# Starting the modulation strips at the tenth instead of the sixth unit of a hybrid encoder's first layer

## Chip, cores and metric

The kernel runs on one core of a Trainium2 chip. The metric is device time in microseconds (us), from the start of the program to its end. TensorE (PE in the rows) does the matmuls; PEld is its weight load, VectorE is DVE, ScalarE is ACT, GpSimd is POOL, and SP is the sequencer whose queue issues nearly all DMAs.

## What is computed

A trunk of two layers over 1024 tokens of width 1024. Layer A is a gated DeltaNet mixer (chunked recurrence, 16 value heads of 128), layer B is attention with forget gates. Each layer is normalised and modulated by three vectors, shift, scale and gate, that come from the conditioning vector `c`. Cut to what matters here:

```python
cond = silu(c)
for i in range(2):
    mod = cond @ ada_w[i] + ada_b[i]            # ada_w[i] is 1024 x 3072
    shift, scale, gate = split(mod, 3)
    h = rmsnorm(x, norm_w[i]) * (1 + scale) + shift
    y = gdn_mixer(h, ...) if i == 0 else fox_mixer(h, ...)
    x = x + gate * y
return rmsnorm(x, final_norm_w)
```

Shift and scale of layer A are needed at once. The gate of layer A is needed first in layer A's output projection; shift and scale of layer B when its norm starts; the gate of layer B only at the kernel's end.

## The kernel before

**Units.** Layer A is worked in 16 units: two halves of 512 tokens, and in each half eight groups of two value heads. `proj_all` runs over the units. In each it projects k, q and two v tiles, and from the second group of a half on also two z tiles of the group before (four in the last group). A projection tile (`proj_tile`) is 24 matmuls of 128x512: the eight parts of the depth, three products each (high times high, high times low, low times high), since every operand is kept as a rounded high part and a remainder. Behind the projections run, for several units at once, the convolution, transposes, the inversion of triangular blocks (`invert_blocks`, `invert_merge`, partly by way of DRAM: tiles `lb`, `lr`, `rb`, `rmat`), the recurrence (`chain`) and `finish`, which stores the unit's output to `og_d` and `ogl_d`.

**Weights.** In the first half the weights are loaded raw and split by ACT (`whi`, line 337) and DVE (`wlo`, line 340), and all but the first three tiles are stored to DRAM (`wc`, line 809). In the second half those 45 tiles are read back ready (line 418). Between the halves `load_norm` splits the second half's activations. The output projection `out_proj_a` splits its own weights again and loads its rows `ohi` and `olo` (line 450) four steps ahead.

**Strips.** `ada_all` computes what is left of the modulation in eight strips of 512 columns: two for the gate of layer A, two each for shift, scale and gate of layer B. A strip (`ada_strip`, lines 271 to 315) loads a piece of the bias (line 273) and eight pieces of `ada_w` of 128x512 into the two buffers `nx` (line 279), and sums them on DVE into one `nh` buffer, weighted by the conditioning column (line 284 for the first, line 286 for the other seven, line 290 for the bias). Then matmuls with a column of ones sum over the partitions into a bank `mm` of PSUM, one of the two that the projections use as well. Strips of shift and scale are copied to `scol` and `gcol` (line 304); strips of a gate go through `nh` (line 313) to `gate_d` in DRAM (line 315).

**Order.** PE's order is written out by hand: a planner, `Flow`, keeps a clock of its own, and generators yield how long they want to wait. Whoever is due and has the lowest priority number goes on. The strips have priority 6, the projections 9; a strip yields `ADP` = 3500 ns after each of nine loading steps and four times that before its matmuls, so its length in the planner's time doesn't depend on where it runs. The other engines' orders, SP's queue included, are made by the scheduler from the program's order and the priorities. What starts the strips is one condition:

```python
def ada_all():
    yield from hold(lambda: done["kp"] >= AD0 + 1)
    ...
    for _ in range(2):
        nc.vector.tensor_copy(al([P, KT], "nx", 2), ts[AD0]["k"][:, 0, 0:KT])
    for l, cl in strips:
        yield from ada_strip(...)
```

`done["kp"]` is raised when a unit's k tile has been projected. The two small copies (line 1283) make the first two loads wait for that tile on the chip too.

Of the kernel before, what the change touches and what calls it, by code (L numbers as in the profile page):

```python
# [88 lines left out]
Y_N2 = 8500  # L89
Y_N3 = 8500  # L90
ADP = 3500
AD0 = 5
R_AD = 600
R_AS = 2500
R_OA = 1150
# [100 lines left out]
def tile_trunk(  # L196
# [154 lines left out]
    def hold(ok):  # L351
        while not ok():
            yield 300
# [177 lines left out]
    with ExitStack() as sa:  # L531
# [744 lines left out]
        def ada_all():  # L1276
            yield from hold(lambda: done["kp"] >= AD0 + 1)
            def al(shape, name, bufs):
                t = at([P, D], name, bufs) if name == "nx" else at([P, 512], name, bufs)
                return t[0 : shape[0], 0 : shape[1]]  # L1280
# [4 lines that stand above are left out]
                yield from ada_strip(  # L1285
                    al, acc_bank, l, cl, 512, ("nx", 2), ("nh", 2), ("nh", 2), 1, ADP
                )
# [656 lines left out]
```

## Time and profile before

| | us |
|---|---|
| median of 3 runs | 1947.3 |
| lowest and highest | 1943.26, 1947.73 |
| the profiled execution, whole | 1945.78 |
| its span (first to last instruction) | 1943.8 |

The profiled execution lies 1.5 us under the median. The rows below are of that execution and count from the start of its span. In them a busy time with (x) gives the number of instructions behind it, PEclk is the mean granted clock of TensorE as a share of 2.4 GHz, and DMA is the mean busy share of 16 DMA engines.

### The profile page before, as it was taken

To read this page: it belongs to the slowest core of one execution; us is meant where nothing else is said; L and a number is where in the kernel's file an instruction comes from. 1 tells how busy PE (TensorE), PEld (TensorE's weight loads), DVE (VectorE), ACT (ScalarE), POOL (GpSimd) and SP (SyncE) were. 2 spreads that over 40 slices of the span, in tenths; PEclk is the share of its full clock that TensorE was granted. 3 is DMA by queue.
4 is the path that set the end of the run, shared out by engine and by line. 5 is a ranking of instruction groups with operands and counts; after the bars stand their busy time and mean duration, and the time that the engine had idled before them with its cause. 6 is when DMAs were issued, how large, how long until landed. Compare 5 with 4: busy or idle time off the path is not lost.

```text
span 1943.8 us, 35877 instructions
## 1 busy us (share of the span) xinstructions
PE 1828.4 (94%) x12888; PEld 1524.4 (78%) x12888; DVE 1328.3 (68%) x3323; ACT 1033.3 (53%) x2674; POOL 367.0 (19%) x402
## 2 busy tenths in 40 slices
PE   6989999999899999999899799999999999999798
PEld 4767778777787878878776578798988988989576
DVE  5677888788786777776665585475665656656764
ACT  4565566565564555555444453465565555655631
POOL 1100110101210110010001244223223132221222
PEclk7889999899999999999999899999999999999899
DMA  7576767667656565454689982112021011112423
GB/s 270 187 229 205 233 210 245 207 212 249 229 181 186 173 192 176 148 172 138 206 268 320 356 303 98 31 48 66 24 65 60 23 60 45 44 55 71 155 87 95
DMA packets 224985, 307.16 MB, mean 158 GB/s; under 512 B 100460, under 2 KB 136940, under 8 KB 224808
## 3 DMA queue, kind: packets, MB, share of 16 engines
q1 hardware_dynamic: 223800, 304.65, 48.4%
q8 instruction: 101, 1.65, 0.4%
q14 instruction: 76, 0.62, 0.1%
q10 hardware_dynamic: 1008, 0.23, 0.1%
HBM read 223.15 MB, written 81.67 MB: 157 GB/s over the span
## 4 chain that ended last, share of the span: by engine, by line
PE 62%; DMA 14%; DVE 13%; ACT 4%; issue 3%; POOL 1%; SPq 1%; ACTq 0%; DVEq 0%; POOLq 0%
PE mm L137 39%; PE lg L137 5%; PE su L137 4%; PE pt L141 3%; PE oT L137 3%; DMA nx<-in_ada_w_dram 3%; PE tr L141 3%; PE ch L137 2%; DVE wlo L340 2%; PE co L137 2%; DVE cv_y L833 2%; DMA ohi<-og_d 2%; DMA rmat<-rb 1%; DMA wraw<-in_wb_dram 1%; ACT whi L337 1%
## 5 line engine op out<-in xcount | busy, mean ns | idle before, releaser
L137 PE MATMUL mm<-ht_h,whi 128*128 128x512 f32 x768 | 342.4, 446 | 0.5 <-DVE nh L313 0.5
L137 PE MATMUL mm<-ht_h,wlo 128*128 128x512 f32 x768 | 305.2, 397 | 0.0
L137 PE MATMUL mm<-ht_l,whi 128*128 128x512 f32 x768 | 304.3, 396 | 0.8 <-POOL ht_l L340 0.8
L137 PE MATMUL mm<-whi,h_h 128*128 128x384 f32 x512 | 186.7, 365 | 0.9 <-DVE kn L1533 0.9
L137 PE MATMUL mm<-wlo,h_h 128*128 128x384 f32 x512 | 172.6, 337 | 0.6 <-POOL wlo L340 0.6
L137 PEld LDWEIGHTS mm<-ht_h,wlo 128*128 128x128 f32 x768 | 146.3, 190 | 33.9
L137 PE MATMUL mm<-whi,h_l 128*128 128x384 f32 x512 | 172.7, 337 | 0.0
L1684 DVE TENSOR_TENSOR ptl<-pt,pth 128x512 fp32r<-128x512 f32 x192 | 106.4, 555 | 92.5 <-ACT pth L1683 90.5
L137 PEld LDWEIGHTS mm<-ht_h,whi 128*128 128x128 f32 x768 | 147.2, 192 | 28.4 <-issue 1.7
L137 PEld LDWEIGHTS mm<-ht_l,whi 128*128 128x128 f32 x768 | 147.7, 192 | 25.2 <-POOL ht_l L340 1.2
L1683 ACT CAST pth<-pt 128x512 fp32r<-128x512 f32 x192 | 91.3, 477 | 139.8 <-PE pt L141 139.0
L833 DVE SCALAR_TENSOR_TENSOR cv_y<-cv_t,conv_h,cv_y 128x512 f32<-128x512 f32 x192 | 144.4, 752 | 17.3 <-ACT cv_y L825 15.6
L1648 ACT ACTIVATE lg<-lg,mx 128x896 f32<-128x896 f32 (+7 forms) x128 | 99.5, 777 | 54.3 <-DVE mx L1640 48.6
L1527 POOL TENSOR_TENSOR rs<-ss,mhalf 128x4 f32<-128x4 f32 x64 | 64.5, 1007 | 330.8 <-DVE ss L1525 325.2
L340 DVE TENSOR_TENSOR wlo<-ht_h,whi 128x512 fp32r<-128x512 f32 x124 | 93.3, 792 | 47.3 <-ACT whi L337 45.1
L337 ACT CAST whi<-ht_h 128x512 fp32r<-128x512 f32 x124 | 70.7, 618 | 86.5 <-PE mm L137 38.6
L137 PE MATMUL mm<-h_h,whi 128*128 128x512 f32 x240 | 100.5, 419 | 0.7 <-DVE wlo L1783 0.3
L137 PEld LDWEIGHTS mm<-whi,h_h 128*128 128x128 f32 x512 | 97.8, 191 | 3.5 <-ACT v L1529 1.2
L137 PEld LDWEIGHTS mm<-wlo,h_h 128*128 128x128 f32 x512 | 97.2, 190 | 2.8 <-POOL wlo L340 0.8
L141 PE MATMUL pt<-ident,lg 128*128 128x128 f32 (+1 forms) x584 | 96.0, 273 | 3.1 <-ACT lg L1648 3.1
L137 PEld LDWEIGHTS mm<-whi,h_l 128*128 128x128 f32 x512 | 96.4, 188 | 0.0
L137 PE MATMUL mm<-h_h,wlo 128*128 128x512 f32 x240 | 94.9, 395 | 0.0
(390 smaller groups left out, 4492.9 us busy)
## 6 DMA issues: line engine op xcount, KB each, us to landing
ht_h<-in_wa_o_dram SPq DMA_DIRECT2D x62, 512.0 KB, 5.2
wc<-whi SPq DMA_DIRECT2D x45, 512.0 KB, 4.5
wc<-wlo SPq DMA_DIRECT2D x45, 512.0 KB, 4.3
wlo<-wc SPq DMA_DIRECT2D x45, 512.0 KB, 4.9
whi<-wc SPq DMA_DIRECT2D x45, 512.0 KB, 3.6
wlo<-in_wa_c_dram SPq DMA_DIRECT2D x35, 512.0 KB, 4.3
nx<-in_ada_w_dram SPq DMA_DIRECT2D x64, 256.0 KB, 3.4
wraw<-in_wb_dram SPq DMA_DIRECT2D x56, 256.0 KB, 2.8
```

Of the source, the lines that this page charges most:

```text
L137: self.nc.tensor.matmul(out, lhsT, rhs, start=start, stop=stop)
L141: self.nc.tensor.transpose(out, src, ident)
L337: nc.scalar.copy(hi, src)
L340: (lo_eng or nc.gpsimd).tensor_tensor(lo, src, hi.bitcast(F32), op=ALU.subtract)
L833: nc.vector.scalar_tensor_tensor(y, raw[:, j : j + HALF], w[:, j : j + 1], y, op0=ALU.mult, op1=ALU.add)
L1527: nc.gpsimd.tensor_tensor(rs, ss, mhalf[:, 0:4], op=ALU.pow)
L1648: nc.scalar.activation(lg, lg, AF.Exp, scale=-1.0, bias=mx[:, hh : hh + 1], accum_out=sums[:, tt : tt + 1],)
L1683: nc.scalar.copy(ph_[:, cs], pp[:, cs])
L1684: nc.vector.tensor_tensor(pl_[:, cs], pp[:, cs], ph_[:, cs].bitcast(F32), op=ALU.subtract)
```

## The change

`AD0` goes from 5 to 9. The strips start when the k tile of the tenth unit (the second of the second half) has been projected, and not that of the sixth. What a strip does, the strips' order and their pace stay as they are.

```diff
 ADP = 3500
-AD0 = 5
+AD0 = 9
 R_AD = 600
```

## Rows read from the trace of the kernel before

**Rows 1.** The page: span, and the busy time of the busiest engine

```profile
span 1943.8 us, 35877 instructions
PE 1828.4 (94%) x12888; PEld 1524.4 (78%) x12888; DVE 1328.3 (68%) x3323; ACT 1033.3 (53%) x2674; POOL 367.0 (19%) x402
```

**Rows 2.** By stretch: length, busy PE, PEld, DVE, ACT, POOL; PEclk, DMA, GB/s

```profile
152.00:325.00 173.00, 166.87 (x1523) 136.53 (x1522) 140.08 (x398) 107.54 (x317) 20.11 (x39) 0.99 0.67 215
274.00:325.00 51.00, 49.21 (x464) 40.24 (x462) 41.94 (x119) 35.09 (x104) 5.11 (x13) 1.00 0.76 237
325.00:562.00 237.00, 221.13 (x1941) 179.60 (x1940) 194.36 (x479) 140.96 (x417) 33.86 (x47) 0.96 0.68 220
562.00:785.00 223.00, 216.44 (x1941) 176.35 (x1940) 168.38 (x469) 117.29 (x363) 24.11 (x33) 0.99 0.61 187
785.00:946.00 161.00, 159.45 (x1447) 130.08 (x1446) 113.41 (x318) 87.16 (x273) 13.11 (x19) 1.00 0.45 137
946.00:1010.00 64.00, 58.73 (x474) 47.20 (x473) 35.19 (x70) 30.14 (x79) 4.63 (x3) 0.92 0.87 285
1010.00:1100.00 90.00, 74.42 (x329) 57.63 (x328) 51.11 (x88) 37.45 (x84) 12.75 (x10) 0.97 0.97 333
```

**Rows 3.** The strips: loads, sums, matmuls and copies of gates, first and last start

```profile
L279 SPq DMA_DIRECT2D nx<-in_ada_w_dram x64: 327/333/1427, 325.7 to 754.0; - x64
nx<-in_ada_w_dram SPq DMA_DIRECT2D x64, 256.0 KB, 3.4
L286 DVE SCALAR_TENSOR_TENSOR nh<-nx,cond,nh x56: 733/748/780, 331.4 to 758.3; 128x512 f32<-128x512 f32 x56
L137 PE MATMUL mm<-nh,ones x8: 590/590/591, 380.1 to 790.4; 128*1 128x512 f32 x8
L313 DVE COPY nh<-mm x4: 669/671/671, 381.5 to 791.8; 1x512 f32<-1x512 f32 x4
```

**Rows 4.** Timeline of DVE: the k tiles of the sixth and tenth unit

```profile
L840 DVE SCALAR_TENSOR_TENSOR k<-cv_t,cv_y x1: 692/692/692, 324.8 to 324.8; 128x512 f32<-128x512 f32 x1
561.38 0.69 DVE L840 SCALAR_TENSOR_TENSOR k<-cv_t,cv_y 128x512 f32<-128x512 f32 x1
```

**Rows 5.** DVE's busy time by stretch, of line 286 alone, then line 290

```profile
325.00:562.00 237.00, 20.93 (x28) 0.96 0.68 220
562.00:790.00 228.00, 20.93 (x28) 0.99 0.61 188
325.00:562.00 237.00, 2.71 (x4) 0.96 0.68 220
```

**Rows 6.** DVE and POOL busy by stretch, of the splits of line 340 alone

```profile
325.00:562.00 237.00, 34.66 (x50) 5.50 (x4) 0.96 0.68 220
562.00:785.00 223.00, 5.47 (x8) 0.00 (x0) 0.99 0.61 187
```

**Rows 7.** Three short stretches of units 6 to 10 at a lower PEclk

```profile
346.00:357.00 11.00, 10.05 (x78) 7.75 (x81) 9.67 (x23) 5.74 (x22) 2.57 (x1) 0.53 0.66 231
421.00:429.00 8.00, 6.06 (x49) 5.18 (x50) 6.44 (x26) 4.28 (x16) 0.00 (x0) 0.57 0.48 180
595.00:599.00 4.00, 3.50 (x11) 2.89 (x12) 3.77 (x15) 3.87 (x15) 0.00 (x0) 0.57 0.60 230
```

**Rows 8.** PE's longest waits from 325 to 562: total us, times, longest

```profile
PE su L137 <- DVE tmat L1223: 3.6, 4, 2.2
PE tr L141 <- ACT rmat L1218: 3.0, 1, 3.0
```

**Rows 9.** Waits of SP's queue at the strips' loads, 321 to 800

```profile
SPq L279 <- DMA nx<-in_ada_w_dram: 24.6, 18, 3.5
SPq L279 <- DVE nh L286: 24.0, 31, 3.1
```

**Rows 10.** Two short stretches of the output projection, columns as in rows 2

```profile
980.00:995.00 15.00, 15.00 (x92) 12.10 (x91) 9.72 (x18) 6.42 (x17) 2.98 (x2) 1.00 0.72 219
1085.00:1100.00 15.00, 5.41 (x23) 4.18 (x23) 5.23 (x11) 5.23 (x11) 2.60 (x3) 0.79 1.04 405
```

**Rows 11.** PE's waits at the output projection's row loads, 946 to 985

```profile
PE mm L137 <- DMA ohi<-og_d: 4.9, 2, 2.7
```

## Prediction

> **What bounds the kernel now.** I read the page first: PE is busy for 94% of the span, DVE for 68% [rows 1]. So time can only come out of what PE still loses, and that is read by stage. The view by stretch gives it: length less PE's busy time is idle time, and a granted clock under 1.00 is lost time beside it. The stretches are cut at the edges that the change moves: 325, where the strips start, right behind the k tile of the sixth unit [rows 3, 4]; 562, the k tile of the tenth unit [rows 4]; about 790, where the strips end [rows 3]; 946, where the output projection begins.
>
> From 325 to 562 PE is idle for 237 - 221.1 = 15.9 us [rows 2]. The clock is down in two places, 11 us at 0.53 and 8 us at 0.57 [rows 7], which loses 11 x 0.47 + 8 x 0.43 = 8.6 us more (the mean clock of 0.96 in rows 2 agrees: 9.5). Together 24.5 us. From 785 to 946, with neither strips nor many splits, PE is idle for 1.6 us of 161 at full clock [rows 2]. PE's waits say what is late in the first of these stretches: not weights or strips but DVE and ACT work of the recurrence and the inversion (tmat, rmat) [rows 8]. These are short operations that stand in line behind others; DVE is busy for 194.4 of 237 us there (82%), against 113.4 of 161 (70%) from 785 on [rows 2]. Part of that DVE line is the strips, and part the splits of weights, 34.7 us up to 562 and only 5.5 us in the 223 us behind [rows 6].
>
> **The change part by part.** *What moves.* Of eight strips, four run before 562 and four behind it: 28 sums of line 286 in either stretch, 20.9 us each [rows 5]. With four bias additions (2.7 us [rows 5]) some 24 us of DVE's work leave the first stretch, besides four first products and small copies of under 1 us each. On SP's queue 32 loads of 256 KB leave it, with the 0.33 us that issuing one takes and the waits in front of them. POOL and ACT have nothing of it. On PE a strip is two to four short matmuls (0.59 us each for a gate [rows 3]), the same in either place: nothing.
>
> *What the first half gains.* The strips' four units are compared with stretches without strips before them, where splits of weights run too. From 152 to 325: 6.1 us idle and a clock of 0.99, so 1.7 us more, 7.8 us in 173; for 237 us that makes 10.7 and a gain of 24.5 - 10.7 = 13.8. That stretch still holds the norm of the second half's tokens; its last 51 us, from 274, lose 1.8 us, which for 237 us is 8.3 and a gain of 16.2. By PE's instructions per us [rows 2]: 1941/237 = 8.19 with strips, 1523/173 = 8.80 and 464/51 = 9.10 without; the 1941 would take 220.5 or 213.3 us, a gain of 16.5 or 23.7. I take **16 us**, where three of the four stand close together. From below: if a strip costs here only what it costs in the second half (next paragraph), the gain is 4 x 1.6 = 6.4. From above: 23.7.
>
> *What the second half pays.* The first four strips now fall where the last four were, units ten to thirteen, and change nothing there. The next three fall into 785 to 946. The price of one: from 562 to 785 PE is idle for 6.6 us and loses 4 x 0.43 = 1.7 at a low clock [rows 2, 7], 8.3 in all; at the rate of 785 to 946 (1.6 in 161) it would be 2.2. So four strips cost 6.1, 1.5 each; by instructions, 1941/8.99 = 215.9 against 223, so 1.8 each. Three at 1.6: **4.8 us**. The bounds: nothing, since DVE has 30% free; or 3 x 4 = 12, if each costs what it costs in the first half (16 / 4).
>
> *Where the last strip falls.* Strips five to eight took from 562 to 792, 57 us each [rows 3]. Starting at 562 - 16 = 546, eight of them end near 1002. The output projection then starts near 946 - 16 + 5 = 935, so the eighth strip loads from about 945 on, within the projection's first 60 us; the trace of before shows no strip there. Its price has two parts. First, DMA: up to eight loads, 2.1 MB. In 946 to 1010 the queues move 285 GB/s and are busy for 87% [rows 2]; at that rate 2.1 MB take 7.4 us if nothing gives way, and nothing if they fit into the free share (13% of 64 us is 8 us; 980 to 995 is busy for 72% only [rows 10]). PE waits for row loads there already, 4.9 us [rows 11]. I take 3 us, nearer to the free share, since the loads of a strip spread over some 20 us. Second, the bank: the strip is of a gate, and from its matmul at 790.0 to the end of the copy at 792.5 [rows 3] an `mm` bank is held for 2.5 us. The output projection holds both banks for 16 steps at a time and then needs both again, so between 0 and 2.5 us; I take 1.5. Together **4.5 us**, between 0 and 10.
>
> The Trainium skill, "DMA: Bandwidth & Descriptors", section "Where 436 GB/s comes from", puts what one core gets from HBM at about 358 GB/s; by it 2.1 MB more in a full stretch would cost an estimated 5.9 us, and the sum below would be 3.8 us in place of 6.7. The trace shows 405 GB/s from 1085 to 1100 [rows 10], so the limit doesn't hold as stated here.
>
> *Waits.* None is added, but the strips' loads stand in SP's queue, which is in order. They held it for 24.6 + 24.0 us over eight strips [rows 9], 6.1 us a strip. In the second half the ready-made weights and the inversion's small transfers stand behind them, in the output projection the row loads. For the former it is in the 1.6 us above, for the latter it is the second rival. The strips have time: layer A's gate is ready near 546 + 114 = 660, well before 935; shift and scale of layer B near 890, before its norm. What is late next in the first half are the splits, and the same DVE and ACT operations with less in front of them.
>
> *The sum.* -16 + 4.8 + 4.5 = **-6.7 us**. The profiled execution took 1945.8, so 1939.1 for one like it; it lies 1.5 us under the median of the runs, so against the median **1940.6**. About 0.3% (5.8 us) is what a measurement of this kernel can tell from no change, so the forecast lies just beyond that.
>
> **Rivals.** (1) *The first half's stalls aren't the strips'.* Units six to ten also hold four z tiles in unit eight and the splits of the second half's activations, and the waits of rows 8 are for the inversion. Then the gain is the lower bound, 6.4: -6.4 + 4.8 + 4.5 = +2.9, 1950.2. For it: no wait of PE there names a strip's sum. Against: unit five, with the same splits and no strip, loses a third.
>
> (2) *The output projection pays, and the kernel is slower.* The eighth strip's loads get into SP's queue between row loads that are only four steps ahead. PE then waits for the 6.1 us that a strip holds the queue, and such waits lower the clock: in 946 to 1010 it is at 0.92, 5.1 us lost, beside 4.9 us of waiting [rows 2, 11], so about as much again. With DMA's 7.4 and the bank's 2.5 that is 22, and -16 + 4.8 + 22 = +10.8, 1958. It decides from 16 - 4.8 + 5.8 = 17 us on for this one strip. For it: DMA at 87 to 97% and a PE that waits for it. Against: by 945 half of the burst of the start is over. The limit of the Trainium skill's page named above ("DMA: Bandwidth & Descriptors", same section) points this way, but not so far.
>
> (3) *The gain is larger.* The first half reaches the rate of unit five (23.7), and the last strip hides in DMA's free share: -23.7 + 4.8 + 0 = -18.9, 1928.4. For it: unit five is the nearest neighbour. Against: 51 us are a short sample.
>
> (4) *The strips don't leave the line but change it.* PE's order is written out again from the planner's clock; if new waits come up elsewhere for those that go, the sum is near nothing, 1947.
>
> **How the numbers follow.** Forecast 0.46 (its own range is 1933 to 1946, so 0.33 of it faster, 0.13 the same); rival 1 0.18 (0.12 the same, 0.06 slower); rival 2 0.18, slower; rival 3 0.13, faster; rival 4 0.05, the same. Faster 0.46, the same 0.30, slower 0.24. The range of 8 in 10 takes in most of rival 3 and of rivals 1 and 2 up to half of the second's excess: 1929 to 1953.
>
> **What would show it.** Right: line 279 starts near 546 and ends near 960 to 975; the stretch between the k tiles of units six and ten is near 221 us, with DVE's share near 75% and at most one short stretch of half clock; 785 to 946 has 4 to 6 us of idle PE in place of 1.6. Wrong: that first stretch still at 230 us or more (rival 1); waits for ohi of over 10 us, or for an `mm` bank, in the first 60 us of the output projection (rival 2); the stretch at 214 (rival 3).

## The result and the profile after

The changed kernel takes 1958.6 us (median of 5 runs, 1951.2 to 1962.7), the kernel before 1945.7 us (median of 5 runs) beside it: a ratio of 1.0056 with an interval from 1.0035 to 1.0077, so 0.56% slower. Measured side by side once more, later, they came out 0.87% apart (1.0069 to 1.0105). The prediction was 1940.6 us and faster; the measured time lies above its range.

The page says where not to look: PE's busy time hardly changed [rows 1], so what was added is waiting and clock.

```profile
span 1957.3 us, 35882 instructions
PE 1834.7 (94%) x12888; PEld 1527.3 (78%) x12888; DVE 1333.3 (68%) x3323; ACT 1031.3 (53%) x2674; POOL 362.1 (19%) x402
```

The strips' loads now run from 547 to 992, where they ran from 326 to 754 [rows 3]; the last gate's copy (line 313) starts at 1033.9 and not at 791.8. The last line is the store of the output projection's result, whose last start was 1196.2 in the trace of before.

```profile
L279 SPq DMA_DIRECT2D nx<-in_ada_w_dram x64: 328/333/1032, 546.9 to 992.4; - x64
L313 DVE COPY nh<-mm x4: 669/672/679, 602.7 to 1033.9; 1x512 f32<-1x512 f32 x4
L526 SPq DMA_DIRECT2D x_d<-ht_l x8: 319/330/418, 1033.2 to 1212.6; - x8
```

How far the kernel is ahead or behind is read at one operation of each unit, the last step of the k tile (line 840) in DVE's timeline. The tenth unit's, which stood at 561.38 [rows 4], and the sixteenth's, which stood at 891.58:

```profile
545.52 0.68 DVE L840 SCALAR_TENSOR_TENSOR k<-cv_t,cv_y 128x512 f32<-128x512 f32 x1
...
900.42 0.69 DVE L840 SCALAR_TENSOR_TENSOR k<-cv_t,cv_y 128x512 f32<-128x512 f32 x1 [0.78 <-ACT cv_t L837]
```

So the new kernel is 15.9 us ahead at the tenth unit and 8.8 us behind at the sixteenth: it loses 24.7 us on the way, 12.5 of them up to the fourteenth unit (785 in before, 782 in after). At the last store of the output projection it is 16.4 us behind, at the end of the span 13.5. The 15.9 is one trace: in fifteen traces of kernels with no strip before the tenth unit (this one and those below, without one that is 54 us late from its start on) that tile stands between 542.1 and 551.0, which is 10 to 19 us ahead.

The same by stretch (columns as in [rows 2]; the edges are the same k tiles, and 960 on is the output projection):

```profile
273.00:328.00 55.00, 51.03 (x469) 41.14 (x468) 42.50 (x119) 35.43 (x105) 5.22 (x13) 1.00 0.69 224
328.00:546.00 218.00, 209.15 (x1921) 171.50 (x1920) 168.78 (x431) 139.88 (x413) 29.72 (x47) 1.00 0.61 197
546.00:782.00 236.00, 222.08 (x1950) 180.28 (x1948) 175.46 (x480) 118.01 (x371) 21.65 (x34) 0.98 0.59 181
782.00:901.00 119.00, 111.39 (x973) 91.71 (x974) 85.11 (x226) 58.60 (x185) 10.05 (x15) 0.96 0.56 173
960.00:1024.00 64.00, 60.27 (x422) 48.25 (x422) 40.78 (x78) 29.28 (x75) 4.63 (x3) 0.95 0.94 314
```

From 328 to 546 PE is idle for 8.9 us at full clock (before: 15.9 idle and 8.6 for the clock). From 546 to 782 it is idle for 13.9 us and the clock is at half in three stretches of 3.4 us, 5.1 us lost: 19.0 together, where before lost 8.3. From 782 to 901 it is 7.6 idle and one stretch of 10.2 us at half clock, 12.7 together, where the like stretch of before (785 to 892) lost 1.6. DVE is busy for 74 and 72% in these two; in the first half before it was 82%, so DVE's busy share alone doesn't say where PE stalls.

PE's waits from 546 to 960 (us in total, times, longest): the recurrence's state update, 1.0 us in before's 562 to 946, has become the first.

```profile
PE ch L137 <- DVE state L1095: 12.9, 6, 4.3
PE su L137 <- DVE tmat L1248: 3.6, 2, 2.9
PE tr L141 <- ACT rmat L1218: 3.5, 2, 1.9
```

DVE's own waits there: the strips' sums for their loads. In before's second half, with four of the eight strips, they are 10.9 us in 10 waits, for all eight 20.2 in 18; so they hardly grew.

```profile
DVE nh L286 <- DMA nx<-in_ada_w_dram: 22.5, 21, 3.0
```

SP's at the same loads: for the landing of the load before in the buffer, for a sum, and at the end of a strip for the copy behind its matmul.

```profile
SPq L279 <- DMA nx<-in_ada_w_dram: 19.6, 14, 4.3
SPq L279 <- DVE nh L286: 14.8, 21, 1.3
SPq L279 <- DVE scol L304: 14.1, 2, 7.6
```

The longest of PE's waits shows how these hang together in this trace. First DVE's timeline (start, length), then PE's, then the clock:

```profile
793.25 0.16 DVE L965 TENSOR_TENSOR wn<-wn,rk 128x8 f32<-128x8 f32 x1
796.38 0.75 DVE L286 SCALAR_TENSOR_TENSOR nh<-nx,cond,nh 128x512 f32<-128x512 f32 x1 [2.97 <-DMA nx<-in_ada_w_dram]
...
799.20 0.74 DVE L286 SCALAR_TENSOR_TENSOR nh<-nx,cond,nh 128x512 f32<-128x512 f32 x1
799.86 0.60 DVE L1095 SCALAR_TENSOR_TENSOR state<-state,g_ex,co 128x128 f32<-128x128 f32 x2
```

```profile
795.88 0.39 PE L137 MATMUL mm<-ht_h,wlo 128*128 128x512 f32 x1
800.60 1.19 PE L137 MATMUL ch<-state,k 128*128 128x256 f32 x2 [4.33 <-DVE state L1095]
```

```profile
799.90:810.10 10.20, 9.50 (x85) 7.48 (x86) 6.95 (x16) 4.35 (x15) 0.00 (x0) 0.50 0.60 158
```

DVE stands for 2.97 us at a sum whose load hasn't landed; the state update is behind it in DVE's order, and PE waits for that 4.33 us, of which the late load can be at most 2.97 (other operations and one more sum stand in between). Around the end of that wait PE's granted clock falls to 0.50, the lower level of 1.2 GHz, for 10.2 us. Wait and clock together cost near 9 us.

It isn't a single case. Of the six waits for the state update, four, with 11.3 of the 12.9 us, have such a late sum less than 6 us before them. The second trace of the same kernel has late sums before the waits at the same four places; its longest:

```profile
617.62 0.75 DVE L286 SCALAR_TENSOR_TENSOR nh<-nx,cond,nh 128x512 f32<-128x512 f32 x1 [3.19 <-DMA nx<-in_ada_w_dram]
...
619.69 1.18 PE L137 MATMUL ch<-state,k 128*128 128x256 f32 x2 [4.06 <-DVE state L1095]
```

This suggests a theory: strips cost by sums that wait in DVE's queue. It is tested below, and doesn't hold as the whole.

In the output projection the row loads are waited for less than before (4.9 us for `ohi`, [rows 11]); columns as above, 946 to 985:

```profile
PE mm L137 <- DMA olo<-ogl_d: 2.0, 1, 2.0
PE mm L137 <- DMA ohi<-og_d: 0.4, 1, 0.4
```

### The profile page after: what moved, and what is told of

It is laid out like the page before. It is cut to its first block, busy times and chain, and to the rows that moved or that the text cites. A ratio compares the mean times of both kernels' runs of the same rounds, so it can differ in the third digit from the quotient of the medians.

```text
span 1957.3 us, 35882 instructions
## 1 busy us (share of the span) xinstructions
PE 1834.7 (94%) x12888; PEld 1527.3 (78%) x12888; DVE 1333.3 (68%) x3323; ACT 1031.3 (53%) x2674; POOL 362.1 (19%) x402
## 5 line engine op out<-in xcount | busy, mean ns | idle before, releaser
L137 PEld LDWEIGHTS mm<-wlo,h_h 128*128 128x128 f32 x512 | 97.3, 190 | 2.2 <-POOL wlo L340 0.2
```

What stands on the lines that cost most here:

```text
L137: self.nc.tensor.matmul(out, lhsT, rhs, start=start, stop=stop)
```

## The experiments

Each ratio is to the kernel before, run beside it on the same chip, with its 95% interval; 0.1% is 1.9 us. Runs of one kernel on one chip spread by 0.3 to 0.4% to either side, and one profile can differ from the next by 7 us (the two spans of the changed kernel are 1957.3 and 1964.1), so sizes are taken from the ratios, places from the traces. The same pair of kernels came out at 1.0056 and at 1.0087: a difference of two ratios that is below some 0.3% says nothing. Rows of waits are from 546 to 960 (us in total, times, longest) unless it is said otherwise. The edits are to the kernel after unless it is said otherwise.

**No strips.** Takes the whole cost of the strips out.

```diff
-for l, cl in strips:
-    yield from ada_strip(...)
+g = al([1, 512], "nh", 2)
+nc.vector.memset(g, 0.5)
+for l in range(2):
+    for c in range(2):
+        nc.sync.dma_start(gate_d[l : l + 1, c * 512 : c * 512 + 512], g)
+nc.vector.memset(scol[1], 0.1)
+nc.vector.memset(gcol[1], 1.0)
```

> The changed kernel with no strips at all: no loads of ada_w, no sums, no matmuls of strips; the gates and layer B's shift and scale are constants, so the output is not the reference's. It is the floor: before less this is what eight strips cost when begun at the sixth unit, after less this what they cost when begun at the tenth. By the prediction's prices (16 + 6 for before) about 1924. If strips cost in the second half what the second half lost in the changed kernel (25 us from the tenth unit's k tile to the sixteenth's, 8 more in the output projection), about 1925 as well, with the first half like the changed kernel's (221 us from the sixth to the tenth k tile) and the second like that of before without its strips (53 us per unit).

Measured: 0.9951 (0.9935 to 0.9968). The eight strips cost 0.49%, some 9.6 us, started at the sixth unit, and 1.05% (20.5 us), by the second measurement 1.36% (26.5 us), started at the tenth. The tenth k tile is 11.4 us ahead of before and the sixteenth 11.5: the second half without strips runs as long as before's did with four of them.

**Sums without loads.** Every strip adds up the first two pieces again; 62 of 64 loads are gone, all sums, matmuls and copies stay.

```diff
-w = alloc([P, width], ...)
-nc.sync.dma_start(w, ada_w[...])
-ws.append(w)
+if len(fixed) < 2:
+    w = alloc([P, width], ...)
+    nc.sync.dma_start(w, ada_w[...])
+    fixed.append(w)
+ws.append(fixed[kk % 2])
```

> The changed kernel with all sums and matmuls of the strips, in the same order for PE's planner, but only two pieces of ada_w are loaded, and every sum reads one of these two; the output is not the reference's. No sum can wait for a load any more. Theory 'queue' (a sum that waits for its load holds DVE's queue, the state update stands behind it, PE waits and its clock falls): the second half is whole again, 1930 to 1936, and PE's waits for the state update (12.9 us from 546 to 960) fall under 4. Theory 'work' (the sums' own 0.75 us each in front of the state update are enough): 1950 to 1958, waits for the state update of 9 us or more. Theory 'order' (the place of the strips in PE's order, or the bank they hold, is what costs): 1950 to 1958, with other waits.

Measured: 0.9968 (0.9950 to 0.9985). 56 sums of 0.75 us, the matmuls, the banks and PE's rewritten order cost 0.17% together, 3.3 us. The other 0.88% (17 us; 1.19% by the second measurement) comes with the 62 loads. Theory 'queue' is met in PE's waits for the state update (3.6 us), but not in the rest: the second half isn't whole again. In this trace it still takes 343.8 us from the tenth to the sixteenth k tile, 13.6 more than in before, and PE has another long wait:

```profile
PE su L137 <- DVE tmat L1198: 7.2, 2, 6.8
```

**Loads without sums.** Of each strip's eight products only the last is taken; all 64 loads stay.

```diff
-if k == 0:
-    nc.vector.tensor_scalar(acc, ws[0], cond[:, 0:1], None, op0=ALU.mult)
-else:
+if k == KT - 1:
+    nc.vector.tensor_scalar(acc, ws[k], cond[:, 0:1], None, op0=ALU.mult)
+elif False:
```

> The changed kernel with all 64 loads of ada_w and the strips' matmuls, but of each strip's eight products only the last is taken, so 56 operations of DVE are left out; the output is not the reference's. Theory 'queue': little waits in DVE (8 of 64 places are left), 1928 to 1938. Theory 'work': the same range. Theory 'order', or loads that hold SP's queue or DMA: still 1948 to 1958. Against the kernel without loads it tells what loads alone cost: under 4 us if SP and DMA have room.

Measured: 1.0094 (1.0065 to 1.0124), no faster than with the sums, though 56 DVE operations are gone. With no sum between them the loads follow one another, and SP stands at them for 97.3 us in place of 19.6; the inversion's transfers, which are behind them on that queue, come later. SP's waits:

```profile
SPq L279 <- DMA nx<-in_ada_w_dram: 97.3, 45, 4.4
...
SPq L1157 <- DMA lb<-d: 16.5, 10, 4.4
```

and DVE's, for what those transfers bring (4.7 us for `lr` in after and 14.9 without strips; 18.0 and 20.1 for `rmat`, so only part of these waits is the loads'):

```profile
DVE xtmp L1167 <- DMA lr<-lb: 23.7, 7, 6.6
DVE tmat L1194 <- DMA rmat<-rb: 23.0, 10, 6.5
```

So the loads can cost this much with 56 of the sums gone. But this kernel also crowds them, so it doesn't say what they do in after.

**The kernel before without loads.** The same edit to the kernel that starts at the sixth unit.

> The kernel before (strips from the sixth unit) with all sums and matmuls, but only two pieces of ada_w loaded; the output is not the reference's. It splits what strips cost in the kernel before (0.49% by the kernel without strips) into loads and sums. If loads are the price there too: 0.995 to 0.997. If in the first half it is DVE's work, as the prediction had it: 0.998 to 1.000, with the stretch from the sixth to the tenth k tile still 10 us longer than in the kernel without strips.

Measured: 1.0030 (1.0008 to 1.0053). Started at the sixth unit, the loads cost nothing by the whole time; without them the kernel is even 0.3% slower. Against no strips, the sums cost 0.79% there (15.4 us), and 0.17% from the tenth unit on. Side by side:

| ratio to before | with loads | without loads | the loads' part |
|---|---|---|---|
| strips from the sixth unit | 1 | 1.0030 | -0.30% |
| strips from the tenth unit | 1.0056, 1.0087 | 0.9968 | +0.88%, +1.19% |

By these whole times, moving the sums is worth 0.62%, 12 us, and moving the loads costs 1.2 to 1.5%. The trace of before without loads puts it elsewhere (tenth and fourteenth k tile; the sixth is at 326.88):

```profile
556.12 0.68 DVE L844 SCALAR_TENSOR_TENSOR k<-cv_t,cv_y 128x512 f32<-128x512 f32 x1
...
787.93 0.68 DVE L844 SCALAR_TENSOR_TENSOR k<-cv_t,cv_y 128x512 f32<-128x512 f32 x1
```

From the sixth to the tenth k tile it takes 229.2 us, 7.4 less than with loads and 5.7 more than without strips, where 10 was expected; so the loads do cost there. What is gained is lost again from the tenth to the fourteenth, 231.8 us against 223.1 with loads. The parts don't add up as prices, and why that second stretch is slower without loads isn't shown.

**Only the first four strips**, those of the units ten to thirteen; the last four, for scale and gate of layer B, are left out.

```diff
-for l, cl in strips:
+g = al([1, 512], "nh", 2)
+nc.vector.memset(g, 0.5)
+for c in range(2):
+    nc.sync.dma_start(gate_d[1:2, c * 512 : c * 512 + 512], g)
+nc.vector.memset(gcol[1], 1.0)
+for l, cl in strips[:4]:
```

> The changed kernel with only the first four strips, which run beside units ten to thirteen; gate and norm scale of layer B are constants, so the output is not the reference's. Against the kernel without strips (0.9951) it prices four strips where the prediction had them cost 1.5 us each: 0.998 by that price, 1.002 if they cost 3.5 us each as the changed kernel's trace has it on the mean over its second half, 0.995 if the cost is all in the later ones.

Measured: 1.0026 (1.0006 to 1.0045), 0.75% over no strips. The first four cost 14.6 us, some 5 us either way, and the other four 6 to 12. The trace has it in the same place: 232.3 us from the tenth to the fourteenth k tile, against 219.9 without strips and 223.1 in before, where the last four strips run beside the same units.

**One unit earlier.** `AD0 = 8`.

> The strips begin one unit earlier, at the ninth unit (AD0 = 8), all else as in the changed kernel; the last strip is then over at about the start of the output projection. Theories 'queue' and 'work': the second half loses as much per strip, the output projection some 5 to 8 us less: 1950 to 1953. Theory 'order' (a matter of how the strips' steps fall against the recurrence): anything, as far as 1940 or 1960.

Measured: 1.0027 (1.0008 to 1.0046), between the kernels that start at the sixth and at the tenth.

**A faster pace.** `ADP = 3000` with `AD0 = 9`: all loads are issued by 910, before the output projection.

> The changed kernel with a strip's pace of 3000 in place of 3500 ns, so that a strip takes some 7 us less in the planner's time and the eight are over some 50 us earlier, before the output projection's rows are loaded. The result is the reference's. If the second rival (the last strip in the output projection) is what makes the changed kernel slower: 0.997 to 1.001. If the price is that of the strips beside units ten to sixteen: 1.003 to 1.007.

Measured: 1.0078 (1.0056 to 1.0101), as slow as after. No load falls into the output projection, so the last strip's loads there aren't needed for the loss. But the loss has moved: in this trace units ten to sixteen take 13.8 us more than in before (24.7 in after), and the stretch from the sixteenth k tile to the last store 13.7 more (7.6 in after), with no strip loading in it.

```profile
L279 SPq DMA_DIRECT2D nx<-in_ada_w_dram x64: 327/333/531, 552.3 to 909.9; - x64
```

**Thirty us later.** `yield 30000` in the planner's time ahead of the first strip.

> The changed kernel, with the strips begun 30 us later in the planner's time, half a unit after the tenth k tile, so that every strip falls half a unit later against the recurrence; the last one ends in the output projection. The result is the reference's. Theory 'order' (it matters where a strip's steps fall within a unit): 0.004 or more from 1.0056, in either direction. Theories 'in-order queues' and 'traffic': 1.004 to 1.008, a little more than the changed kernel because of the output projection.

Measured: 1.0126 (1.0088 to 1.0165). With loads until 1015 PE waits from 910 to 1180 for its rows (first number, us):

```profile
PE mm L137 <- DMA olo<-ogl_d: 11.9, 8, 3.3
...
PE mm L137 <- DMA ohi<-og_d: 4.6, 3, 2.8
```

That doesn't show that the output projection pays for the strip: the kernel with the faster pace, which loads nothing there, waits as long (after itself 10.5 us).

```profile
PE mm L137 <- DMA olo<-ogl_d: 12.8, 9, 4.0
...
PE mm L137 <- DMA ohi<-og_d: 5.0, 4, 1.8
```

By the ratio, theory 'order' is met: it is 0.4 to 0.7% above the two measurements of the changed kernel, and above the range of the other theories. Where a strip's steps fall within a unit may matter, then; no run separates it from the output projection.

**An eighth of the bytes.** The 62 loads stay in their places, 64 columns wide and not 512; the sums take the rest from the first two pieces.

```diff
+else:
+    nc.sync.dma_start(fixed[kk % 2][:, 0:64], ada_w[layer, kk * P : (kk + 1) * P, col : col + 64])
```

> As the kernel without loads, but each load left out is back at an eighth of its width (64 of 512 columns, 32 KB) into the buffer that the sum reads whole: all waits of SP for a free buffer and of DVE for a landed load are back, the bytes are not. The output is not the reference's. Theory 'in-order queues': most of the loss is back, 1.002 to 1.006 of before. Theory 'traffic': 0.995 to 0.999.

Measured: 1.0020 (1.0003 to 1.0038), 0.52% over the sums without loads. About half of the loads' price stays with an eighth of their bytes, so bytes alone don't make it. But the sums also wait for the loads half as long as in after, so this kernel doesn't tell waits from bytes:

```profile
DVE nh L294 <- DMA nx<-in_ada_w_dram: 10.6, 8, 2.3
```

**The bytes without the waits, twice.** As sums without loads, but each load left out becomes a transfer that no sum uses. First from `ada_w` to DRAM, waiting for nothing:

```diff
+tr_d = dram.tile([P, width], F32, name="tr_d", tag=f"tr_d{layer}_{col}_{kk}")
+nc.sync.dma_start(tr_d, ada_w[layer, kk * P : (kk + 1) * P, col : col + width])
```

> As the kernel without loads (0.997 of before), but in place of each load left out the same 256 KB of ada_w is copied from DRAM to DRAM, each copy to a place of its own: the bytes, the issues and SP's place for them are back, but nothing waits for them and they wait for nothing. The output is not the reference's. Theory 'traffic' (the loads' bytes hold up the recurrence's and the weights' transfers): 1.003 of before or more, like the changed kernel. Theory 'in-order queues' (what costs is that a load holds SP until its buffer is free, and that a sum holds DVE until its load has landed): 0.995 to 0.999.

Measured: 1.0284 (1.0249 to 1.0320), and it answers nothing: the scheduler put all 62 at the start, where they delay everything by 54 us.

```profile
L286 SPq DMA_DIRECT2D tr_d<-in_ada_w_dram x62: 490/491/677, 1.7 to 54.1; - x62
```

Then 256 KB of the current unit's k tile to DRAM, which can't be issued before that tile is there:

```diff
+nc.sync.dma_start(tr_d, ts[done["kp"] - 1]["k"].rearrange("p c t -> p (c t)"))
```

> As the kernel without loads (0.997 of before), but in place of each load left out 256 KB of the current unit's k tile go from the buffer to a scratch place in DRAM, issued by SP at the strip's step: bytes and issues are spread as the strips' are, nothing waits for them, and what they wait for is long done. The output is not the reference's. Theory 'traffic': 1.002 to 1.006. Theory 'in-order queues': 0.995 to 0.999.

Measured: 0.9963 (0.9946 to 0.9980), the same as without them.

```profile
L286 SPq DMA_DIRECT2D tr_d<-k x62: 319/524/997, 542.9 to 890.9; - x62
```

62 transfers of 256 KB on SP's queue, in groups behind each k tile, cost nothing measurable when nothing waits for them. They are writes; the loads are reads, and that difference wasn't tried.

**Another queue.** `nc.gpsimd.dma_start` in line 279.

> The changed kernel with the strips' 64 loads issued from GpSimd's queue in place of SP's, same bytes, same buffers, same sums. SP no longer stands at them; DVE still waits for them, and GpSimd's small operations of the recurrence now stand behind them. If what costs is SP's queue held by the strips (row loads, weights and the inversion's transfers behind): 0.995 to 1.000 of before. If it is DVE held by sums whose load is late: 1.002 to 1.007, with DVE's waits at line 286 of 15 us or more from the tenth unit on. Theory 'traffic': 1.004 to 1.007.

Measured: 1.0087 (1.0054 to 1.0120). SP is rid of the loads and nothing is gained. DVE still waits for them, and GpSimd stands at them instead:

```profile
POOL nx L279 <- DVE nh L286: 67.1, 29, 5.8
...
POOL nx L279 <- DVE scol L304: 19.1, 2, 11.4
```

**Three pieces ahead.** Four half buffers in place of the two, so that a load has two more steps to land.

```diff
-w = alloc([P, width], ...)
+if not slots:
+    for _ in range(2):
+        w2 = alloc([P, 2 * width], *wtag)
+        slots.extend((w2[:, 0:width], w2[:, width : 2 * width]))
+w = slots[nslot[0] % 4]
+nslot[0] += 1
...
-yield pace
+yield pace if kk >= ahead - 1 else 0
...
-al, acc_bank, l, cl, 512, ("nx", 2), ("nh", 2), ("nh", 2), 1, ADP
+al, acc_bank, l, cl, 512, ("nx", 2), ("nh", 2), ("nh", 2), 3, ADP
```

> The changed kernel with the two nx buffers cut into four halves (a piece needs half a buffer), so that the loads run three pieces ahead and not one; the strip's length in the planner's time stays the same, and so do bytes, sums and issues. The result is the reference's. Theory 'in-order queues': loads are there when the sums come, and buffers are free when the loads come: DVE's waits at line 286 fall from 22.5 us to under 8, 0.995 to 1.000 of before, faster than before. Theory 'traffic': 1.003 to 1.007. If the strips' sums (DVE's work) were the cause after all: 1.003 or more too, with few waits at line 286.

Measured: 1.0046 (1.0024 to 1.0069). DVE's waits for the loads fall from 22.5 to 5.0 us (546 to 960), but the time by 0.1 to 0.4% only. PE's waits are now these:

```profile
DVE nh L293 <- DMA nx<-in_ada_w_dram: 5.0, 3, 2.4
```

```profile
PE ch L137 <- DVE state L1102: 5.8, 5, 1.8
PE su L137 <- DVE tmat L1230: 3.6, 5, 0.9
PE su L137 <- DVE tmat L1201: 3.4, 2, 3.1
```

So the chain shown above is at most a part. The waits for the inversion's blocks (`tmat`) needn't be the loads' doing: sums without loads have 7.2 us in the last of these lines. The same with the loads on ACT's queue:

> The changed kernel with the nx buffers in four halves and loads three pieces ahead, and these loads issued from ACT's queue in place of SP's: the bytes are all there, SP no longer stands at a strip's load, and neither DVE nor ACT should wait long for one. The result is the reference's. Theory 'in-order queues' in its wider form (SP's hold and DVE's wait each suffice, so that taking one away helps little): 0.996 to 1.000 of before. Theory 'traffic' (bytes): 1.003 to 1.006, as with four halves alone (1.0046).

Measured: 1.0041 (1.0011 to 1.0071). And on GpSimd's:

> The changed kernel with the nx buffers in four halves, loads three pieces ahead, and these loads issued from GpSimd's queue: SP and ACT don't stand at a strip's load, DVE's waits at line 286 are short, and all bytes are there. The result is the reference's. If the loss is that of queues in order, whichever: 0.996 to 1.000 of before, faster than both kernels. If GpSimd's own small operations (the powers that the recurrence and the norms wait for) now stand behind the loads: 1.003 to 1.008 with waits of DVE for GpSimd above those of the changed kernel.

Measured: 1.0051 (1.0029 to 1.0072). There neither DVE nor SP stands much at the loads. PE waits for the state for 7.0 us, and for `tmat` in the same line for 7.4, as it does in the sums without loads.

**Half as many loads.** Pieces in pairs, 32 loads of 512 KB, with the sums as in after.

```diff
-nc.sync.dma_start(w, ada_w[layer, kk * P : (kk + 1) * P, col : col + width])
+if kk % 2 == 0:
+    w2 = nxpair()              # both nx halves: 128 x 2 x 512
+    nc.sync.dma_start(
+        w2, ada_w[layer, kk * P : (kk + 2) * P, col : col + width].rearrange("(m p) f -> p m f", p=P))
```

> The changed kernel with two pieces of ada_w in one load of 512 KB, into the two nx buffers of 1024 columns: 32 loads in place of 64, the same bytes, the same sums; SP stands at a strip's load half as often, and a sum finds its piece landed one step earlier. The result is the reference's. Theory 'in-order queues': 0.998 to 1.002. Theory 'traffic': 1.004 to 1.007.

Measured: 1.0078 (1.0058 to 1.0099). Their number isn't the price either. Nor are DVE's waits for them alone: they are 6.2 us here, against 22.5 in after.

**The change once more.**

> The changed kernel once more, on the chip of the following runs, to compare with directly: 1.0035 to 1.0077 of before, its first interval.

Measured: 1.0087 (1.0069 to 1.0105), with the same shape: 12.6 us ahead at the tenth k tile, 10.6 behind at the sixteenth.

**By place.** Us between the same k tiles, and from the last one to the last store of the output projection; one trace each, and the two of the changed kernel show how far traces differ:

| | sixth to tenth | tenth to sixteenth | sixteenth to last store |
|---|---|---|---|
| before | 236.6 | 330.2 | 304.6 |
| after, two traces | 218.4, 221.8 | 354.9, 353.4 | 312.2, 314.0 |
| no strips | 223.5 | 330.1 | 309.4 |
| sums without loads | 225.2 | 343.8 | 302.7 |
| before without loads | 229.2 | 338.4 | 303.1 |
| a faster pace | 223.2 | 344.0 | 318.3 |
| thirty us later | 220.7 | 351.2 | 321.6 |

The whole times say that the loss goes with the loads. By place it is less simple: sums without loads still lose 13.6 of the 24.7 us from the tenth to the sixteenth k tile, and what makes that kernel fast is as much the stretch behind. There, traces without a strip's load differ by 15 us (302.7 to 318.3), so nothing of a few us can be read from it.

No version here that does the whole work is faster than the kernel before; without strips at all it would be 0.5%.

## Why the prediction was wrong

*What bounds the kernel, and the first half: right in size.* The gain was put at 16 us, the stretch at near 221 with DVE near 75% and no more than one stretch at half clock. The trace has 15.9 us, 218.4, DVE at 77% and none. That the gain meets 16 so closely is luck: the second trace has 12.6, the others 10 to 19. Since the stretch is 218 to 225 us in all fifteen traces, the first rival (230 or more) falls. What the gain consists of is less clear than the prediction had it, which spoke of DVE's line above all: by the trace of before without loads, 7.4 us of the stretch go with the loads; by whole times the gain is the sums'.

*What the second half pays: this is the step that failed*, in both parts. "The first four strips now fall where the last four were, units ten to thirteen, and change nothing there" gave 0; the trace has 12.5 us there, and timing gives four strips 14.6 us over none. "Three at 1.6: 4.8 us" gave the next; the trace has 12.2 up to the sixteenth unit, just beyond the upper bound of 12. The price of 1.6 came from what PE lost in a stretch of before beside one without strips. For before it was not too low: by single traces the same units take 223.1 us with the last four strips and 219.9 with none, 3.2 us for four. With the first four strips beside them they take 235.5 (237.4 in the second trace). So a strip had no price that could be carried from one place to another, not even between strips of the same size beside the same units. And the lower bound's reason, "DVE has 30% free", failed in kind: DVE is 72 to 74% busy here as well, and PE loses 31.7 us.

*The waits.* "For the former it is in the 1.6 us above" made the loads' waits on SP's queue part of that price. SP's waits at line 279 did not grow (19.6 + 14.8 + 14.1 us up to 960, against 24.6 + 24.0 and smaller ones in before, [rows 9]), and moving them off SP gains nothing. Nor did DVE's for the loads, 22.5 us against 20.2 for all eight strips. What grew is PE's wait for the state update, 12.9 us against 4.5 in before (3.5 from 325 to 562 and 1.0 behind it): DVE stood at late loads as long in either kernel, but in the new place the state update stood behind them more often. The prediction spoke of SP's queue and had no term for DVE's.

*The last strip: later than said, and its price not shown.* The loads end at 992 and not at 960 to 975, the last strip at 1034 and not at 1002, since a strip took 61 us and not before's 57. The bank is waited for 1.1 us (1.5 in the sum). From the sixteenth k tile to the last store 7.6 us are lost, against 4.5; but without strips 4.7 are lost there too, and traces without a strip's load there differ by 15 us.

*The sum in the trace's numbers:* -15.9 + 12.5 + 12.2 + 7.6, less 2.9 in layer B, where traces differ by 4 us anyhow, is +13.5 us of span, where the prediction had -16 + 0 + 4.8 + 4.5.

*The rivals.* The second named 1958 and came out at the measured time for another reason, so that is luck. Its place was the output projection; its sign, waits for `ohi` of over 10 us in the first 60, is 1.0 us in the trace, and a kernel whose loads end before is as slow. Missing was the rival that held: the strips cost the second half more than they give the first. The third falls with the size of the first half's gain. The fourth, a changed order, isn't settled by any run: PE's rewritten order costs little without the loads (sums and order together 0.17%), but DVE's order changes with every variant.

*What stays open.* Shown, by whole times: the strips cost 0.5% from the sixth unit on and 1.05 to 1.36% from the tenth, and without their loads 0.17% there. A strip's loads in the output projection aren't needed for the loss (the faster pace has none), and 62 writes that nothing waits for don't bring it. Shown by two traces, for a part: a sum that waits for its load holds the state update, and PE's clock falls at three of these waits in either trace. Removing most of DVE's waits for loads gave back 0.1 to 0.4% of 0.9 to 1.2% with four half buffers, and nothing with loads in pairs; taking the loads off SP's queue nothing; both together no more. So why the loads cost this much there stays open. It can be reads under way beside the inversion's transfers, where the strips' steps fall within a unit, or how the scheduler lays out the orders of DVE and SP around the loads (against its base, each of four variants looked at has 130 to 190 of DVE's 3323 operations elsewhere, and under 40 of PE's 12888). Nor is it shown why taking the loads out of before helps up to the tenth unit and hurts behind it.

## What to carry to other kernels

What a moved step will cost in its new place can't be read from the idle time of a stretch in which its like happened to run: take the step out, then only its loads, then only its sums, and time each in both places; and look by place as well, since parts that are timed alone needn't add up. DVE's free share said nothing here about a step that waits for a load and holds others behind it. And time the kernel without the step first: here that bounded all that any placement could gain at 0.5%, less than the step's loads cost in the wrong place.

## What was not expected of the hardware

Sixty-two writes of 256 KB that nothing waits for cost nothing measurable (0.9963 with, 0.9968 without), while as many loads of 32 KB that sums wait for cost 0.5%. Leaving out 56 DVE operations made nothing faster (1.0094), in a kernel whose loads then crowd. Taking 62 loads out of the kernel before made it slower (1.0030, interval 1.0008 to 1.0053): with PE busy for 94%, less work elsewhere can come with a loss as large as the changes under study. That a shifted order is the reason isn't shown. Four strips beside the same four units cost 3 us in one kernel and 16 to 18 in another.
